# Splitting f32 weights on the engines instead of by summing transfers, in a two-part network kernel

## The chip, the cores and the metric

One core of a Trainium2 chip runs the whole program. Its engines are TensorE (PE, with PEld for weight loads), VectorE (DVE), ScalarE (ACT), GpSimd (POOL) and SyncE (SP), each with an instruction queue that is worked off in order. The metric is the device time of one execution in microseconds, as the median of several runs.

## The reference, cut to what matters

Everything is float32, 256 tokens of width 1024. Two hybrid layers (a gated recurrence beside sparse attention) are followed by one mixer layer (RWKV7 beside a forgetting attention) and a mixture of experts.

```python
def hybrid_layer(x, norm_g, w_in, ..., w_out):          # twice
    h = rms_norm(x, norm_g)
    z = h @ w_in
    ...
    y_a = rg_lru(causal_depthwise_conv(rg_x, conv_w, conv_b), ...)
    y_a = y_a * jax.nn.silu(rg_gate)
    y_b = nsa(q, k_c, v_c, k_s, v_s, k_w, v_w, br_gate, ...)
    y_b = y_b * jax.nn.silu(nsa_gate)
    y = jnp.concatenate([y_a, y_b], axis=-1)
    return x + y @ w_out

def second_block(x, ...):                               # once
    h = rms_norm_2(x, norm_mix_w[l])
    p = h @ w_in[l]
    y_rw = rwkv7_mixer(...); y_fox = fox_mixer(...)
    x = x + jnp.concatenate([y_rw, y_fox], axis=-1) @ w_out[l]
    h = rms_norm_2(x, norm_ffn_w[l])
    return x + hierarchical_moe(h, ...)                 # 16 groups of 4 experts
```

## The kernel before, in words

The dense projections (`h @ w_in`, `y @ w_out`) are computed from split operands: a float32 weight w is turned into hi, which is w rounded to the type that PE reads fast, and lo = w - hi. `mm3_steps` then sums three products, hi by hi, lo by hi and hi by lo (L304). The activations are split by `split` and `split_ps`. What this case is about is where the weights are split.

A weight block is 128 partitions by 2048 columns, 1 MB, half of a chunk of `w_in` or `w_out`. There are 50: blocks 0 to 15 for the first hybrid layer (12 of `w_in`, 4 of `w_out`; the third chunk has only 1120 columns to a half), 16 to 31 for the second, 32 to 49 for the mixer. A split block (hi and lo, 2 MB) lies in one of seven numbered places of SBUF (`block`); `RING` lists the places that blocks go through in turn, and a block's transfer waits until PE has read the block that had its place before. Everything else lies in `arena`, from which `alloc` gives regions out (names in `LONG` from the top).

`weights_steps` is called when a chunk comes up and issues transfers up to a block or two beyond the one it takes:

- Blocks 0 to 3 are loaded as they are by SP into `raw` (L254), ACT writes hi (CAST, L277, in four pieces), and POOL and DVE in turn subtract to make lo (L280).
- From block 4 on, a transfer that POOL issues writes hi and rounds on the way (L256); ACT writes lo = -hi (L286); and two further transfers from POOL read the weights from HBM a second time and add them onto lo (L291, `accum_op=OP.add`).

`hybrid` interleaves the recurrence (`rg_part`) with the attention in small steps on PE (`self.step`). The scan and attention of `mixer` are interleaved in the same manner (the scan's small matmuls are L1057). Softmax work of both attentions is at L801 to L814 on DVE. The mixer's parameters (`par2`, L833) come by SP while the second hybrid layer ends, and DVE scales them at L860 to L863.

The order of instructions on each engine is set by a scheduler from the program, so a step may stand among others' on its queue. `moe` streams the experts' weights, 2 MB at a time, by SP into "slots" (`fill`, L1557 and L1542): the seven places as they come free, and regions of the arena. The first few slots are taken while the mixer still works (`early_slot`), and each waits until what lay there has been read.

Of the kernel before, what the change touches and what calls it, by code (L numbers as in the profile page):

```python
# [35 lines left out]
E_W2, E_G2, E_E8, E_END = 0, 512, 1024, 1536  # L36
ARENA = 24512
BLOCK, NB = 4096, 7
RING = (6, 2, 3, 0, 1)
WS = 2  # L40
# [45 lines left out]
class Net:  # L86
    def __init__(self, ctx, tc, A, norm):
        self.tc, self.nc, self.A = tc, tc.nc, A
        nc = tc.nc
# [6 lines left out]
        self.pool = pool  # L96
        self.blocks, self.loaded, self.nload, self.ntake, self.ndone = [], [], 0, 0, 0
        self.x = self.t([128, 2, 1024], "x")
        for t in range(2):
# [50 lines left out]

    LONG = ("x", "ident", "nh", "cst", "sub", "oneb", "ones", "chunk1", "cmo", "par2", "eh", "small", "fz", "PE",
            "bon", "keyg", "lg", "rss", "gt", "BK", "UV")
# [85 lines left out]
    def plan(self, blocks):  # L238
        self.blocks += blocks
        if self.nload == 0:  # L240
            self.issue(4)

    def issue(self, upto):

        while self.nload < min(upto, len(self.blocks)):
            name, idx, off, n = self.blocks[self.nload][:4]
            b = self.block(RING[self.nload % 5], "w", F32R, 2)[:, :, :n]
            src = self.A[name][idx][:, off:off + n]
            if self.nload < 4:

                if self.nload % 2 == 0:
                    raw = self.block(5 if self.nload else RING[4], "raw", F32, 2)
                src = raw[:, self.nload % 2, :n]
                self.nc.sync.dma_start(src, self.A[name][idx][:, off:off + n])  # L254
            else:
                self.nc.gpsimd.dma_start(b[:, 0], src)  # L256
            self.loaded.append((b, src))
            self.nload += 1

    def weights(self, name, k, pin=False):  # L260
        return run_all(self.weights_steps(name, k, pin))

    def weights_steps(self, name, k, pin=False):


        assert self.blocks[self.ntake][0] == name
        self.issue(self.ntake + 3 - self.ntake % 2)
        i = self.ntake
        b, src = self.loaded[i]
        self.ntake += 1  # L270
        hi, lo = b[:, 0], b[:, 1]
        m = hi.shape[-1]
        r = lambda a: a.rearrange("p (k n) -> p k n", k=k)
        if i < 4:
            for q in range(4):
                sl = slice(q * m // 4, (q + 1) * m // 4)
                a = self.S.copy(hi[:, sl], src[:, sl])  # L277
                if pin:
                    self.tc.keep_in_program_order(a)
                (self.V if q % 2 else self.G).tensor_tensor(lo[:, sl], src[:, sl], hi[:, sl].bitcast(F32), OP.subtract)  # L280
                yield 0
            return r(hi), r(lo)
        n = 4 if m > 1024 else 1
        for i in range(n):
            sl = slice(i * m // n, (i + 1) * m // n)
            a = self.S.activation(lo[:, sl], hi[:, sl].bitcast(F32), AF.Copy, scale=-1.0)  # L286
            if pin:
                self.tc.keep_in_program_order(a)
            if n == 1 or i % 2:
                sl = slice((i - 1) * m // n if i else 0, (i + 1) * m // n)  # L290
                self.G.dma_start(lo[:, sl], src[:, sl], accum_op=OP.add)  # L291
            yield 0
        return r(hi), r(lo)

    def mm3(self, *a):
# [155 lines left out]
    pin = False  # L451
# [270 lines left out]
    def rg_part(self, l, hT, yT, sgn):  # L722
# [27 lines left out]
        self.gated = True  # L750
        tr, ti, a, tq, gt = (self.t([128, 4, 256], n) for n in ("tr", "ti", "a", "tq", "gt"))

# [14 lines left out]
        yield from gates()  # L767
        self.free("xp")

        def out_weights():  # L770
# [71 lines left out]
    def mixer(self, w0, more):  # L842
        nc, T, V, S, G = self.nc, self.T, self.V, self.S, self.G
# [6 lines left out]
        gt = self.t([128, 2, 512], "gt")  # L850
# [22 lines left out]
        lo = self.t([128, 2, 256], "lo", at=12304)  # L873
# [17 lines left out]
        lw, L, ta, k = (self.t(A4, n, at=a) for n, a in (("lw", 4608), ("L", 8192), ("ta", 9216), ("k", 1024)))  # L891
# [327 lines left out]
        for cc in range(4):  # L1219
            i, q = cc // 2, cc % 2  # L1220
# [50 lines left out]
        if more:  # L1271
            self.moe_memory()
            self.moe_params()
            self.route_init()
            self.slots += [self.block(i, "slot", F32) for i in (4, 2, 3)]
            self.fill()
# [400 lines left out]
    def moe(self, out):  # L1677
        ktd = self.t([128, 128], "ktd")
        self.slots += [self.block(i, "slot", F32) for i in ((0, 1, 5) if self.early else range(7))]
        self.fill()  # L1680
# [138 lines left out]
def model(tc, A, out, upto=9, only=None):  # L1819
    with ExitStack() as ctx:  # L1820
# [16 lines left out]
        if only is None:  # L1837
            net.hybrid_params()
            w0 = net.chunk("w_in")
            for l in range(min(2, upto)):  # L1840
                if l == 1:
                    if upto > 2:
                        net.plan_mixer()
                w0 = net.hybrid(l, w0, net.norm_step if l + 1 < upto else None)
            net.free("par", "cl", "ncl", "hb")
        if upto < 3:
# [33 lines left out]
```

## Time and profile before

| what | value |
|---|---|
| median of 3 runs | 1508.16 us (1506.3 to 1509.79) |
| the profiled execution: its own time, its span | 1520.82 us, 1519.1 us |
| PE busy | 1217.5 us, 80% |
| DVE, ACT, POOL busy | 423.2, 316.2, 148.0 us |
| HBM read | 507.83 MB |
| of which through POOL's queue | 90.65 MB |
| mean granted clock of PE | 0.873 of full speed |

Times within the profile belong to the profiled execution, which took 12.66 us longer than the median run. A line L304 is a line of the kernel; an idle time in brackets stands ahead of the instruction that it precedes, with what ended it.

### The profile page before, as it was taken

Reading aid. Unit: us, or ns where it says so; the run is one execution under the profiler, and the core shown is the slowest. Engines: PE = TensorE matmul, PEld = TensorE weight load, DVE = VectorE, ACT = ScalarE, POOL = GpSimd, SP = SyncE. Lnnn points to the kernel's source line nnn. Section 1 sums busy time; section 2 is a strip of 40 time slices with the busy share of each in tenths; the row PEclk is TensorE's granted clock in tenths of the full one; section 3 lists DMA queues with packets and bytes.
Section 4 is the critical chain, followed back from the end, with each engine's and each line's share of the span. In section 5 each row is a group of like instructions: output and inputs, shape, how many; then the busy total and the mean of one; then the engine's idle time right before and its main releaser. Section 6 shows DMA issues by size and latency. Waiting matters only on the chain.

```text
span 1519.1 us, 20669 instructions
## 1 busy us (share of the span) xinstructions
PE 1217.5 (80%) x8695; PEld 678.3 (45%) x8695; DVE 423.2 (28%) x1250; ACT 316.2 (21%) x748; POOL 148.0 (10%) x201
## 2 busy tenths in 40 slices
PE   6799889889778998976876876877868768768774
PEld 5777677676656685431331331322313313313311
DVE  6546346533525465210110101101101101101010
ACT  4448346736223412000000000000000000000000
POOL 5221322122302300000000000000000000000000
PEclk9979989988899898987987888978878979878897
DMA  8976999749746668999999999999999999999996
GB/s 322 229 190 153 254 281 246 196 129 253 177 99 149 158 230 331 428 427 428 428 428 428 428 428 427 427 428 428 427 428 427 427 429 428 427 429 428 423 408 229
DMA packets 62005, 510.27 MB, mean 336 GB/s; under 512 B 5948, under 2 KB 6076, under 8 KB 34388
## 3 DMA queue, kind: packets, MB, share of 16 engines
q1 hardware_dynamic: 42180, 418.26, 65.7%
q0 software_dynamic: 19728, 90.65, 24.7%
q8 instruction: 70, 1.15, 0.3%
q14 instruction: 27, 0.22, 0.0%
HBM read 507.83 MB, written 1.05 MB: 335 GB/s over the span
## 4 chain that ended last, share of the span: by engine, by line
PE 39%; DMA 33%; DVE 3%; issue 3%; POOL 1%; ACT 0%; POOLq 0%; ACTq 0%; DVEq 0%
DMA slot<-in_wu 19%; DMA arena<-in_wu 12%; PE sc L1608 10%; PE ot L1639 8%; PE tp L1579 8%; PE mm L304 5%; DMA arena<-in_wd 1%; PE tp L1630 1%; DVE arena L1626 1%; PE ot L1057 1%; DMA w<-in_w_in 1%; PE mm L1647 0%; POOL w L291 0%; PE sc L1057 0%; PE sc L1374 0%
## 5 line engine op out<-in xcount | busy, mean ns | idle before, releaser
L1608 PE MATMUL sc<-slot,arena 128*32 128x512 f32 x1424 | 326.6, 741 | 132.5 <-DMA slot<-in_wu 81.4
L1608 PE MATMUL sc<-arena 128*32 128x512 f32 x624 | 187.2, 737 | 61.2 <-DMA arena<-in_wu 37.7
L1608 PEld LDWEIGHTS sc<-slot,arena 128*32 128x32 f32 x1424 | 70.0, 131 | 307.6 <-issue 122.5
L304 PE MATMUL mm<-hT,w 128*128 128x256 f32 (+1 forms) x936 | 142.3, 309 | 4.7 <-DMA w<-in_w_in 3.2
L304 PEld LDWEIGHTS mm<-hT,w 128*128 128x128 f32 (+1 forms) x936 | 127.8, 207 | 17.9 <-issue 9.2
L1579 PEld LDWEIGHTS tp<-arena 128*128 128x128 f32 x512 | 124.3, 334 | 17.9 <-issue 17.9
L1579 PE MATMUL tp<-arena 128*128 128x128 f32 x512 | 128.5, 406 | 2.4 <-DVE arena L1577 2.4
L1639 PE MATMUL ot<-slot,arena 128*32 128x512 f32 x704 | 124.4, 596 | 2.8 <-DMA slot<-in_wd 2.0
L286 ACT ACTIVATE w<-w 128x512 fp32r<-128x512 f32 (+1 forms) x181 | 99.0, 603 | 92.5 <-DMA w<-in_w_in 58.1
L1608 PEld LDWEIGHTS sc<-arena 128*32 128x32 f32 x624 | 40.7, 131 | 166.3 <-issue 76.3
L304 PE MATMUL mm<-w,hT 128*128 128x512 f32 (+1 forms) x432 | 105.1, 396 | 10.7 <-DVE arena L502 4.4
L304 PEld LDWEIGHTS mm<-w,hT 128*128 128x128 f32 x432 | 78.5, 200 | 27.8 <-issue 8.8
L1626 DVE SCALAR_TENSOR_TENSOR arena<-arena,sc 128x512 f32<-128x512 f32 x16 | 11.0, 688 | 265.8 <-PE sc L1608 265.8
L1625 DVE SCALAR_TENSOR_TENSOR arena<-arena,sc 128x512 f32<-128x512 f32 x16 | 11.0, 688 | 265.3 <-ACT arena L1624 265.3
L1649 DVE TENSOR_TENSOR arena<-arena,mm 128x512 f32<-128x512 f32 x64 | 44.0, 688 | 118.2 <-PE mm L1647 118.2
L304 PE MATMUL mm<-w,y 128*128 128x512 f32 x288 | 75.5, 408 | 0.9 <-DVE arena L747 0.9
L1639 PE MATMUL ot<-arena 128*32 128x512 f32 x320 | 71.9, 608 | 3.6 <-DMA arena<-in_wd 3.6
L291 POOL DMA_DIRECT2D w<-in_w_in x67 | 59.5, 946 | 136.5 <-ACT w L286 125.5
L1632 ACT COPY arena<-tp 128x512 f32<-128x512 f32 x16 | 9.4, 586 | 302.7 <-PE tp L1630 302.7
L1644 ACT COPY arena<-ot 128x512 f32<-128x512 f32 x32 | 18.8, 586 | 250.3 <-PE ot L1639 250.3
L1647 PE MATMUL mm<-arena 128*128 128x512 f32 x128 | 64.6, 628 | 1.6 <-ACT arena L1644 1.4
L1624 ACT ACTIVATE arena<-sc 128x512 f32<-128x512 f32 x16 | 9.6, 597 | 261.0 <-PE sc L1608 261.0
(386 smaller groups left out, 1246.8 us busy)
## 6 DMA issues: line engine op xcount, KB each, us to landing
slot<-in_wg SPq DMA_DIRECT2D x47, 2048.0 KB, 31.1
slot<-in_wu SPq DMA_DIRECT2D x42, 2048.0 KB, 33.5
slot<-in_wd SPq DMA_DIRECT2D x42, 2048.0 KB, 35.3
arena<-in_wu SPq DMA_DIRECT2D x22, 2048.0 KB, 33.4
arena<-in_wd SPq DMA_DIRECT2D x18, 2048.0 KB, 34.9
arena<-in_wg SPq DMA_DIRECT2D x17, 2048.0 KB, 32.0
w<-in_w_in POOLq DMA_DIRECT2D x29, 1024.0 KB, 8.7
w<-in_w_in POOLq DMA_DIRECT2D x58, 512.0 KB, 8.8
```

What stands on the lines that cost most here:

```text
L286: a = self.S.activation(lo[:, sl], hi[:, sl].bitcast(F32), AF.Copy, scale=-1.0)
L291: self.G.dma_start(lo[:, sl], src[:, sl], accum_op=OP.add)
L304: ins = self.T.matmul(out, lhsT=lhs[k][a], rhs=rhs[k][b], start=(first and i == 0 and k == 0), stop=(last and i == 2 and k == n - 1))
L1057: ins = T.matmul(o[qd(q, d), h * 32:(h + 1) * 32], lhsT=lhs[qd(q, d), h], rhs=rhs[qd(q, d), h], start=True, stop=True)
L1579: ins = T.matmul(self.rows[k // 4][:, k % 4 * 128:(k % 4 + 1) * 128], lhsT=hv[:, tt, k], rhs=D[:, tt], start=(tt == 0 and k % 4 == 0), sto ...
L1608: T.matmul(dst[32 * j:32 * j + 32], lhsT=XT[:, k, 32 * j:32 * j + 32], rhs=w(j), start=(k == 0), stop=(k == 7))
L1626: V.scalar_tensor_tensor(hid, hid, 0.5, pu, OP.mult, OP.mult)
L1630: T.transpose(ps[:, k * 128:(k + 1) * 128], hw[:, k], self.ident)
L1639: T.matmul(py[h][32 * j:32 * j + 32], lhsT=HT[:, k, 32 * j:32 * j + 32], rhs=w(j), start=(k == 0), stop=(k == 3))
L1644: S.copy(Y[:, cs], py[h])
L1647: T.matmul(pc, lhsT=DT[:, tt * 128:(tt + 1) * 128], rhs=Y[:, cs], start=True, stop=True)
L1649: V.tensor_tensor(xs, xs, pc, OP.add)
```

## The change

Every block is now loaded as it is by SP, into one of the two halves of `raw`, which lies in the arena for the two hybrid layers and in place 6 for the mixer. The load of block i+2 is issued only when the instructions that split block i are there (`nload - ndone < 2`), so it waits until block i's half has been read. hi is made by ACT's CAST in four pieces, except in twelve blocks (`by_dma`: 8 to 13 and 24 to 29), where a transfer from POOL writes it. lo is made by subtraction, two quarters on POOL and two on DVE (in the twelve, three on POOL and one on DVE). No transfer adds. The split blocks go through five places in the hybrid layers and four in the mixer. One region (`gt`) is allocated later, the arena grows to hold `raw` (the room comes from a smaller area for POOL's transfer descriptors), and the order in which places become slots for the experts follows the new ring.

```diff
-ARENA = 24512
+ARENA = 26560
-RING = (6, 2, 3, 0, 1)
+RING, RING2, MIXER = (0, 1, 2, 3, 6), (2, 3, 0, 1), 32
...
+        while self.nload < len(self.blocks) and self.nload - self.ndone < 2:
             name, idx, off, n = self.blocks[self.nload][:4]
...
+            if self.nload == MIXER:
+
+                self.raw = self.block(6, "raw", F32, 2)
+            w = self.raw[:, self.nload % 2, :n]
+            self.nc.sync.dma_start(w, self.A[name][idx][:, off:off + n])
...
+    def issue_upper(self, upto):
+
+        while len(self.upper) < min(upto, len(self.blocks)):
...
+            tag = RING[i % 5] if i < MIXER else RING2[(i - MIXER) % 4]
+            b = self.block(tag, "w", F32R, 2)[:, :, :n]
+            if self.by_dma(i):
+                self.nc.gpsimd.dma_start(b[:, 0], self.A[name][idx][:, off:off + n])
...
-            a = self.S.activation(lo[:, sl], hi[:, sl].bitcast(F32), AF.Copy, scale=-1.0)
...
-                self.G.dma_start(lo[:, sl], src[:, sl], accum_op=OP.add)
+            if not self.by_dma(i):
+                a = self.S.copy(hi[:, sl], w[:, sl])
...
+            (self.V if (q == 3 if self.by_dma(i) else q % 2) else self.G).tensor_tensor(lo[:, sl], w[:, sl], hi[:, sl].bitcast(F32), OP.subtract)
             yield 0
+        self.ndone += 1
+        self.issue()
...
+        return i < 32 and 8 <= i % 16 < 14
...
-            self.slots += [self.block(i, "slot", F32) for i in (4, 2, 3)]
+            self.slots += [self.block(i, "slot", F32) for i in (4, 0, 1)]
...
-        self.slots += [self.block(i, "slot", F32) for i in ((0, 1, 5) if self.early else range(7))]
+        self.slots += [self.block(i, "slot", F32) for i in ((2, 3, 5) if self.early else range(7))]
...
+    nc = bacc.Bacc("TRN2", target_bir_lowering=False, num_devices=1, dynamic_dma_scratch_size=8192)
```

Lines after the change stand one or two further on (L304 is L305, L814 is L816); the load is L251, the rounding transfer L263, ACT's CAST L281 and the subtraction L284. Of these the program has 50 loads (one, in the mixer, of only 64 columns), 12 rounding transfers, 152 CASTs, 112 subtractions on POOL and 88 on DVE.

Three places in the queues follow. POOL's queue at the first hybrid layer, before, for blocks 5 to 9 (w_329, w_331, w_373, w_375, w_447):

```order
L256 DMA w_331<-in_w_in 128x2048 [waits PE_49]
L291 DMA w_329<-in_w_in 128x560 [waits Activation_49] x2
L291 DMA w_331<-in_w_in 128x1024 [waits Activation_49]
L291 DMA w_331<-in_w_in 128x1024 [waits DMASW0_49,Activation_49]
L256 DMA w_373<-in_w_in 128x2048 [waits DVE_49,DMASW1_49,PE_49,Pool_49]
L256 DMA w_375<-in_w_in 128x2048 [waits DVE_49,DMASW2_49,PE_49,Pool_49]
L291 DMA w_373<-in_w_in 128x1024 [waits DMASW3_49,Activation_49]
L291 DMA w_373<-in_w_in 128x1024 [waits DMASW4_49,Activation_49]
L256 DMA w_447<-in_w_in 128x2048 [waits DMASW5_49,PE_49]
L256 DMA w_449<-in_w_in 128x2048 [waits DMASW6_49,PE_49]
```

The same stretch of POOL's queue now (block 5 is w_328, 6 is w_329, 7 is w_376, 8 w_377, 9 w_455, 10 w_457, 11 w_743):

```order
L263 DMA w_377<-in_w_in 128x2048 [waits DVE_49,PE_49,Pool_49]
L284 TENSOR_TENSOR w_328<-arena,w_328 128x280 [waits DMAHW4_49,Activation_49]
L284 TENSOR_TENSOR w_328<-arena,w_328 128x280 [waits Activation_49]
L263 DMA w_455<-in_w_in 128x2048 [waits DVE_49,PE_49,Pool_49]
L284 TENSOR_TENSOR w_329<-arena,w_329 128x512 [waits DMAHW5_49,Activation_49]
L284 TENSOR_TENSOR w_329<-arena,w_329 128x512 [waits Activation_49]
L263 DMA w_457<-in_w_in 128x2048 [waits DVE_49,PE_49,Pool_49]
L284 TENSOR_TENSOR w_376<-arena,w_376 128x512 [waits DMAHW6_49,Activation_49]
L284 TENSOR_TENSOR w_376<-arena,w_376 128x512 [waits Activation_49]
L263 DMA w_743<-in_w_in 128x2048 [waits DVE_49,PE_49,Pool_49]
L284 TENSOR_TENSOR w_377<-arena,w_377 128x512 [waits DMAHW7_49,DMASW0_49]
```

The adding transfers are gone; the subtractions of blocks 5, 6 and 7 now each stand behind a rounding transfer that waits for PE to leave a place.

DVE's queue at the end of the second hybrid layer's attention, before (L860 to L862 scale `par2`; L814 divides the last softmax):

```order
L398 TENSOR_TENSOR arena<-arena,mm_2585 128x512 [waits PE_49]
L806 RECIPROCAL arena<-arena 128x4 [waits Activation_49]
L860 TENSOR_SCALAR arena<-arena 128x14 [waits DMAHW1_49]
L809 TENSOR_TENSOR arena<-arena 128x2 [waits DVE_49]
L809 TENSOR_TENSOR arena<-arena 128x2
L861 TENSOR_SCALAR arena<-arena 128x8
L814 TENSOR_SCALAR arena<-arena 128x128 [waits DVE_49]
L814 TENSOR_SCALAR arena<-arena 128x256
L814 TENSOR_SCALAR arena<-arena 128x128 [waits DVE_49]
L814 TENSOR_SCALAR arena<-arena 128x256
L862 TENSOR_SCALAR arena<-arena 128x4
```

The same place of DVE's queue now (w_2717 is block 31, whose split frees the region that `par2` is loaded into):

```order
L284 TENSOR_TENSOR w_2717<-arena,w_2717 128x512 [waits Activation_49]
L399 TENSOR_TENSOR arena<-arena,mm_2600 128x512 [waits PE_49]
L808 RECIPROCAL arena<-arena 128x4 [waits Activation_49]
L811 TENSOR_TENSOR arena<-arena 128x2 [waits DVE_49]
L811 TENSOR_TENSOR arena<-arena 128x2
L816 TENSOR_SCALAR arena<-arena 128x128 [waits DVE_49]
L816 TENSOR_SCALAR arena<-arena 128x256
L816 TENSOR_SCALAR arena<-arena 128x128 [waits DVE_49]
L816 TENSOR_SCALAR arena<-arena 128x256
L399 TENSOR_TENSOR arena<-arena,mm_2649 128x512 [waits PE_49]
L862 TENSOR_SCALAR arena<-arena 128x14 [waits DMAHW4_49]
```

The division has moved ahead of the instruction that waits for `par2`, and a subtraction of the last block of weights stands ahead of both.

SP's queue at the start of the program, before (`raw` is two tiles of two blocks each):

```order
L100 DMA arena<-in_x 128x1024
L254 DMA raw_70<-in_w_in 128x2048 x2
L254 DMA raw_75<-in_w_in 128x2048 x2
L120 DMA arena<-in_cst 128x1218
L125 DMA arena<-in_par 128x968 [waits DMAHW0_49]
L125 DMA arena<-in_par 128x968 [waits DMAHW1_49]
L521 DMA arena<-in_w_cmp 128x4096 [waits DMAHW2_49]
```

And now:

```order
L101 DMA arena<-in_x 128x1024
L251 DMA arena<-in_w_in 128x2048 x2
L121 DMA arena<-in_cst 128x1218
L126 DMA arena<-in_par 128x968 x2
L251 DMA arena<-in_w_in 128x2048 [waits DMAHW0_49,DMAHW3_49,DVE_49,Pool_49]
L251 DMA arena<-in_w_in 128x2048 [waits DMAHW1_49,DMAHW4_49,DVE_49,Pool_49]
L522 DMA arena<-in_w_cmp 128x4096 [waits DMAHW2_49]
L251 DMA arena<-in_w_in 128x1120 [waits DMAHW0_49,DVE_49,Pool_49]
L251 DMA arena<-in_w_in 128x1120 [waits DMAHW1_49,DVE_49,Pool_49]
```

Two loads of blocks go out at once, and from the third on each waits for the subtractions (DVE and POOL) of the block two before it.

## Rows read from the trace of the kernel before

**Rows 1.** Busy time, clock and transfers in two stretches: us, then each engine's.

```profile
0.00:586.00 586.00, 512.03 (x4885) 404.42 (x4886) 297.36 (x961) 271.56 (x663) 147.98 (x201) 0.91 0.78 208
586.00:1519.00 933.00, 705.43 (x3812) 273.84 (x3811) 125.84 (x289) 44.65 (x85) 0.00 (x0) 0.85 0.99 416
```

**Rows 2.** Timeline of SP: the transfer from which slots load without a break.

```profile
557.96 0.37 SPq L1557 DMA_DIRECT2D slot<-in_wu  x1
```

**Rows 3.** Timeline of PE at four gaps: start, us, instruction [idle before <- releaser].

```profile
28.85 12.76 PE L304 MATMUL mm<-w,hT 128*128 128x512 f32 x48 [3.24 <-DVE arena L502]
...
58.20 1.12 PE L540 MATMUL tp<-arena 128*128 128x128 f32 x4 [5.73 <-DVE arena L410]
...
302.90 1.51 PE L822 MATMUL tp<-arena 128*128 128x128 f32 x6 [5.79 <-DVE arena L814]
...
370.02 0.88 PE L981 MATMUL ot<-arena 128*8 128x256 f32 x2 [3.36 <-ACT arena L921]
```

**Rows 4.** Timeline of ACT ahead of the gap at 58.20, and at 367.54.

```profile
53.40 2.19 ACT L286 ACTIVATE w<-w 128x512 fp32r<-128x512 f32 x4 [7.62 <-DMA w<-in_w_in]
...
367.54 0.63 ACT L286 ACTIVATE w<-w 128x512 fp32r<-128x512 f32 x1 [4.74 <-DMA w<-in_w_in]
```

**Rows 5.** Timeline of DVE ahead of the gaps at 58.20 and at 302.90.

```profile
55.97 0.19 DVE L530 TENSOR_SCALAR arena<-arena 128x48 f32<-128x48 f32 x1 [8.23 <-ACT arena L527]
...
302.17 0.17 DVE L860 TENSOR_SCALAR arena<-arena 128x14 f32<-128x14 f32 x1 [6.08 <-DMA arena<-in_par]
```

**Rows 6.** Groups of instructions by line, 186 to 215 us: busy, mean ns | idle before.

```profile
L304 PE MATMUL mm<-w,hT 128*128 128x280 f32 (+1 forms) x91 | 19.3, 372 | 4.4 <-DMA w<-in_w_in 4.4
...
L304 PE MATMUL mm<-hT,w 128*128 128x256 f32 x19 | 3.3, 316 | 2.6 <-DMA w<-in_w_in 2.1 <-ACT arena L527 0.6
```

**Rows 7.** Groups of PE by line, 402 to 466 us, the scan's matmuls.

```profile
L1057 PE MATMUL ot<-arena 32*32 32x32 f32 x896 | 10.6, 195 | 9.7 <-issue 9.7
...
L1057 PE MATMUL sc<-arena 32*32 32x32 f32 x448 | 6.6, 200 | 7.5 <-issue 7.4
```

**Rows 8.** Busy time in one of the scan's gaps, columns as in rows 1.

```profile
460.50:464.00 3.50, 0.00 (x0) 0.00 (x0) 0.74 (x2) 1.15 (x2) 0.00 (x0) 0.77 1.01 215
```

**Rows 9.** Eight stretches behind such gaps: first, last, and the sum of the eight.

```profile
57.00:62.00 5.00, 3.80 (x18) 3.80 (x19) 3.29 (x12) 2.76 (x6) 2.67 (x4) 0.50 1.03 195
...
462.00:469.00 7.00, 5.00 (x63) 3.69 (x67) 0.69 (x1) 2.78 (x5) 3.09 (x6) 0.53 0.78 142
sum 41.00, PE 34.40 PEld 29.13 DVE 10.45 ACT 9.05 POOL 8.17; mean PE 4.30 PEld 3.64 DVE 1.31 ACT 1.13 POOL 1.02
```

**Rows 10.** Instructions on the tile `raw` (blocks 0 to 3): ns min/median/max, and landing in us.

```profile
L277 ACT CAST w<-raw x16: 610/620/625, 10.6 to 22.7; 128x512 fp32r<-128x512 f32 x16
L280 POOL TENSOR_TENSOR w<-raw,w x8: 1274/1304/1835, 11.3 to 25.5; 128x512 fp32r<-128x512 f32 x8
L280 DVE TENSOR_TENSOR w<-raw,w x8: 678/682/5051, 13.1 to 27.4; 128x512 fp32r<-128x512 f32 x8
...
DMA to landing us min/median/max: 8.4/10.4/14.3
```

**Rows 11.** The page's costliest groups over the span: busy, mean ns | idle before.

```profile
L304 PE MATMUL mm<-hT,w 128*128 128x256 f32 (+1 forms) x936 | 142.3, 309 | 4.7 <-DMA w<-in_w_in 3.2
...
L286 ACT ACTIVATE w<-w 128x512 fp32r<-128x512 f32 (+1 forms) x181 | 99.0, 603 | 92.5 <-DMA w<-in_w_in 58.1
...
L291 POOL DMA_DIRECT2D w<-in_w_in x67 | 59.5, 946 | 136.5 <-ACT w L286 125.5
```

**Rows 12.** Timeline of DVE beside POOL's subtractions and products, and alone.

```profile
22.31 5.05 DVE L280 TENSOR_TENSOR w<-raw,w 128x512 fp32r<-128x512 f32 x1 [1.35 <-ACT w L277]
...
511.49 3.47 DVE L814 TENSOR_SCALAR arena<-arena 128x128 f32<-128x128 f32 x4
...
518.76 1.01 DVE L814 TENSOR_SCALAR arena<-arena 128x128 f32<-128x128 f32 x4
```

**Rows 13.** Timeline of POOL beside the first two of rows 12.

```profile
21.19 3.81 POOL L280 TENSOR_TENSOR w<-raw,w 128x512 fp32r<-128x512 f32 x3
...
512.17 1.27 POOL L1143 TENSOR_TENSOR gn<-gn,arena 128x512 f32<-128x512 f32 x1
```

**Rows 14.** The waits up to 620 us: total us, times, longest.

```profile
POOL w L256 <- PE mm L304: 119.8, 23, 18.1
```

More of the change, by code (lines that the diff above doesn't have):

```diff
@@ L97, in __init__ @@
         self.blocks, self.loaded, self.nload, self.ntake, self.ndone = [], [], 0, 0, 0
+        self.raw, self.upper = self.t([128, 2, 2048], "raw"), []
         self.x = self.t([128, 2, 1024], "x")
@@ L148, in block @@
         return t.rearrange(f"p ({' '.join(ax)}) -> p {' '.join(ax)}", **dict(zip(ax, shape)))
-    LONG = ("x", "ident", "nh", "cst", "sub", "oneb", "ones", "chunk1", "cmo", "par2", "eh", "small", "fz", "PE",
+    LONG = ("raw", "x", "ident", "nh", "cst", "sub", "oneb", "ones", "chunk1", "cmo", "par2", "eh", "small", "fz", "PE",
             "bon", "keyg", "lg", "rss", "gt", "BK", "UV")
@@ L239, in plan, with issue @@
         self.blocks += blocks
[L240 to L245, printed above, removed]
+        self.issue()
+    def issue(self):
+        while self.nload < len(self.blocks) and self.nload - self.ndone < 2:
             name, idx, off, n = self.blocks[self.nload][:4]
[L247 to L257, printed above, removed]
-            self.nload += 1
+            if self.nload == MIXER:
+                self.raw = self.block(6, "raw", F32, 2)
+            w = self.raw[:, self.nload % 2, :n]
+            self.nc.sync.dma_start(w, self.A[name][idx][:, off:off + n])
+            self.loaded.append(w)
+            self.nload += 1
+    def issue_upper(self, upto):
+        while len(self.upper) < min(upto, len(self.blocks)):
+            i = len(self.upper)
+            name, idx, off, n = self.blocks[i][:4]
+            tag = RING[i % 5] if i < MIXER else RING2[(i - MIXER) % 4]
+            b = self.block(tag, "w", F32R, 2)[:, :, :n]
+            if self.by_dma(i):
+                self.nc.gpsimd.dma_start(b[:, 0], self.A[name][idx][:, off:off + n])
+            self.upper.append(b)
     def weights(self, name, k, pin=False):
@@ L263, in weights_steps, with by_dma @@
     def weights_steps(self, name, k, pin=False):
-        assert self.blocks[self.ntake][0] == name
-        self.issue(self.ntake + 3 - self.ntake % 2)
         i = self.ntake
-        b, src = self.loaded[i]
+        assert self.blocks[i][0] == name
+        self.issue_upper(min(i - i % 2 + 3, MIXER) if i < MIXER else i - i % 2 + 2)
+        w, b = self.loaded[i], self.upper[i]
         self.ntake += 1
+        m = w.shape[1]
         hi, lo = b[:, 0], b[:, 1]
[L272 to L277, printed above, removed]
+        for q in range(4):
+            sl = slice(q * m // 4, (q + 1) * m // 4)
+            if not self.by_dma(i):
+                a = self.S.copy(hi[:, sl], w[:, sl])
                 if pin:
                     self.tc.keep_in_program_order(a)
[L280 to L285, printed above, removed]
-            a = self.S.activation(lo[:, sl], hi[:, sl].bitcast(F32), AF.Copy, scale=-1.0)
[L287 to L290, printed above, removed]
-                self.G.dma_start(lo[:, sl], src[:, sl], accum_op=OP.add)
+            (self.V if (q == 3 if self.by_dma(i) else q % 2) else self.G).tensor_tensor(lo[:, sl], w[:, sl], hi[:, sl].bitcast(F32), OP.subtract)
             yield 0
+        self.ndone += 1
+        self.issue()
+        r = lambda a: a.rearrange("p (k n) -> p k n", k=k)
         return r(hi), r(lo)
+    @staticmethod
+    def by_dma(i):
+        return i < 32 and 8 <= i % 16 < 14
     def mm3(self, *a):
@@ L750, in rg_part @@
         self.gated = True
-        tr, ti, a, tq, gt = (self.t([128, 4, 256], n) for n in ("tr", "ti", "a", "tq", "gt"))
+        tr, ti, a, tq = (self.t([128, 4, 256], n) for n in ("tr", "ti", "a", "tq"))
         def gates():
@@ L768, in rg_part @@
         self.free("xp")
+        gt = self.t([128, 4, 256], "gt")
         def out_weights():
@@ L1844, in model @@
                 w0 = net.hybrid(l, w0, net.norm_step if l + 1 < upto else None)
-            net.free("par", "cl", "ncl", "hb")
+            net.free("par", "cl", "ncl", "hb", "raw")
         if upto < 3:
@@ L1868 @@
     from concourse.bass_utils import run_bass_kernel_spmd
-    nc = bacc.Bacc("TRN2", target_bir_lowering=False, num_devices=1)
+    nc = bacc.Bacc("TRN2", target_bir_lowering=False, num_devices=1, dynamic_dma_scratch_size=8192)
     arrays, A = {}, {}
```

## The prediction

> **What bounds the kernel now.** I read the busy times by stage first. Up to 586 us PE is busy 512.0 of 586, and transfers take 0.78 of their time; after it transfers take 0.99 at 416 GB/s and PE 705 of 933 [rows 1]. So there are two programs: dense layers near PE's bound with 74 us of idle PE, and an expert stage bound by its stream. SP's timeline shows where the stream becomes continuous, at 557.96 us [rows 2]. Its first slots wait for the places and regions that the mixer reads last, so whatever ends the mixer earlier starts the stream earlier, and the end follows one to one. What DVE, ACT and POOL do matters only where PE waits for them.
>
> Then I looked at PE's gaps before the experts, and behind each at the engine named. The gap of 5.73 us at 58.20 names DVE [rows 3], but DVE had itself waited 8.23 us for ACT's L527 [rows 5], which stood in ACT's queue behind L286, whose four pieces had waited 7.62 us for a weight transfer [rows 4]. The reader should see that a late weight here stops a queue that other work shares. The second hybrid layer starts with 4.4 + 2.6 = 7.0 us of gaps in front of the projections, nearly all put down to weight transfers [rows 6]. The gap of 5.79 us at 302.90 names DVE's L814; DVE stood 6.08 us in L860, waiting for the mixer's parameters [rows 3, 5]. The gap of 3.36 us at 370.02 names ACT's L921, behind an L286 that waited 4.74 us for weights [rows 3, 4]. In the scan, PE's L1057 loses 9.7 + 7.4 = 17.1 us to nothing that the profile names [rows 7]; in the one gap that I show, PE did nothing for 3.5 us while transfers were busy all the time at only 215 GB/s [rows 8]. Behind such gaps PE's clock stands at its lower level, 1.2 GHz of 2.4 (granted 0.50 to 0.58): eight stretches, 41 us together with 34.4 us of PE work [rows 9].
>
> **The change, part by part, against the profiled execution** (1520.82 us, span 1519.1, 1.7 outside; 12.66 above the median, from which I then take the same difference).
>
> *Removed: the second reading and the two chained transfers.* Before, a block needs a landing, ACT, an issue on POOL and a second landing. ACT gives up 181 L286 (99.0 us) for 136 more CASTs of 0.62 us (84 us), POOL gives up its L291 (59.5 us for 67 of them) [rows 10, 11]. Terms, each with both ends:
> - First layer's start: gaps of 3.24 and 5.73, 8.97 together [rows 3]. The first is DVE's L502 behind a subtraction that took 5.05 us [rows 12]; that can recur, as POOL still subtracts there. The second should mostly go, as ACT's queue no longer stops for a landing that was itself queued behind PE. I take 6 (0 to 9).
> - Second layer's start: 7.0, of which I take 6 (0 to 7): raw loads go out as soon as a half of `raw` is read, not when PE leaves a place.
> - `par2`: the order puts the division ahead of the wait, but the load now goes out only after block 31's split, and L862 still holds DVE afterwards. I take 3 of 5.79 (0 to 5.8).
> - L921: 3 of 3.36 (0 to 3.4), for the same reason as the first two.
> - The scan's unnamed gaps: if they are made longer by the slow adding transfers, some of 17.1 goes. Nothing in the trace says how much; I take 4 (0 to 8.5, half).
> - Clock: the 34.4 us of PE work in rows 9 stood at a mean of about 0.53, so at the upper level they would take 18 and save 16. The gaps don't all go, so half: 8 (0 to 16).
>
> Sum of the gains: 6 + 6 + 3 + 3 + 4 + 8 = 30.
>
> *Added: subtractions.* POOL gets 104 more at 1.30 us, 136 us; DVE 80 more at 0.68, 55 us [rows 10]. Up to 586 us that makes DVE 352 and POOL about 220 of 586, ACT 257 [rows 1], so no engine becomes the bound by its sum. What they cost is where they meet. DVE's subtraction beside three of POOL's took 5.05 us and not 0.68, and DVE's L814 took 3.47 us beside POOL's products and 1.01 without them [rows 10, 12, 13]: 2.46 us lost in one meeting. If none lies on the path the price is nothing, since PE has other steps of the interleaved layers to go on with; if one does, it is 2.46. I take three, one for each layer: 7 (0 to 44, the rival below).
>
> The Trainium skill, "SBUF — State Buffer", section "Who interferes with whom", states this as a rule that speaks against the change: a VectorE instruction with two SBUF inputs contends with a GpSimd instruction that reads SBUF, and for VectorE's 2-port modes it says that the other fully blocks for the whole instruction. By that rule every subtraction on one of the two would wait for one on the other, and the two halves of a split would hardly overlap; the two rows above agree, one of 5.05 us with three on POOL of 3.81 us in all beside it.
>
> *Moved: POOL's order.* The subtractions of blocks 5, 6 and 7 stand behind a rounding transfer that waits for PE to leave a place. Such waits took POOL 119.8 us in 23 times before [rows 14], with L291 behind them. The place of block 8 is that of block 3, which PE leaves when it turns to blocks 4 and 5; block 5 then needs an issue of about 0.9 us (as L291) and two subtractions, while PE still has block 4's products. That is close, so 1.5 us a layer, 3 in all (0 to 8). In the attentions the later places come free a block ahead.
>
> *Moved: loads to SP.* SP's queue is in order, and loads stand behind gains, `w_cmp` and `par2`, which wait little: 1 us (0 to 4). Places, slots and `gt` change names, not the time: the last four blocks of the mixer fill four places as before, and six slots follow them. That costs nothing as long as the stream hides it.
>
> Costs: 7 + 3 + 1 = 11. Net: 30 - 11 = 19 us. Of the profiled execution that gives 1502, of the median 1508.16 - 19 = **1489 us**. With the single ends moved by some third, the likeliest case reaches from 1478 to 1501.
>
> **The rivals.**
> - *Slower by meetings on the shared side of DVE and POOL.* The softmax runs on DVE while POOL subtracts 36 quarters in the two attentions. If every second of them meets DVE on the path, that is 18 x 2.46 = 44 us, against 30 - 4 = 26 of net gain: 1508 + 18 = 1526. It decides from 11 meetings on. For it speak rows 12; against it, that DVE is busy only half of the time in these layers [rows 1] and PE is the engine that waits least.
> - *About the same: two halves of `raw` are too few.* A half is taken for a landing, four CASTs (2.5 us) and the last subtraction (1.3). PE's work per block at a layer's start is 48 matmuls at 142.3 / 936 = 0.152, 7.3 us [rows 11]. At the median landing of 10.4 two halves give a block every 7.1 us, just enough; between median and slowest, at 12.4, every 8.1, 0.8 short, and over the eight blocks at each of three starts 19 us: 1508. At the slowest landing, 14.3, it is 1.75 short, 42 us, and slower [rows 10]. Against it: those four loads were in flight at once beside others, and now only two are.
> - *The whole gain.* All terms at their upper ends (9 + 7 + 5.8 + 3.4 + 8.5 + 16 = 50) less the 4 of POOL and SP: 46, 1462 us. For it speaks that most gaps name one cause; against it, that a gap which goes shows the next one.
>
> **How the numbers follow.** The forecast has 0.60, the whole gain 0.13, too few halves 0.13, meetings 0.14. The time is that of the first: 1489. A range that leaves out the outer half of the whole gain and most of the meetings reaches from 1464 to 1512. A difference below 0.2% (3 us) can't be told from none here. The forecast and the whole gain are faster (0.73); the halves' case, from 1489 to 1531 by its landing, gives 0.05 faster, 0.05 same, 0.03 slower; the meetings 0.01 same and 0.13 slower. Together: 0.78 faster, 0.06 same, 0.16 slower.
>
> **What the profile after would show.** Right: no gap of 5 us at 58, no weight transfer among the waits in front of the second layer's projections, landings of raw blocks of 5 to 9 us, a continuous stream from about 539 us. The clock term is right if the granted clock before the experts rises above 0.91. Wrong by meetings: DVE's L816 or the subtractions with means of twice their 0.25 and 0.68 us, and PE waiting for them in the attentions. Wrong by the halves: ACT's CAST waiting for the transfer of `raw`, and PE for CAST. Wrong altogether if the mixer ends earlier but the stream doesn't, because its slots wait for something else.

## The result, and the profile after

The change made the kernel slower: 1548.26 us (median of four runs, 1539.68 to 1554.25) against 1508.97 for the kernel before on the same chip, a ratio of 1.0259 (95% interval 1.0207 to 1.0311). The forecast was 1489, the range 1464 to 1512.

The first view is SP's timeline again, at the transfer from which slots load without a break ([rows 2] of before had it at 557.96).

```profile
586.84 0.37 SPq L1559 DMA_DIRECT2D slot<-in_wu  x1
```

It comes 28.9 us later, and the span is 28.8 us longer (1547.9 against 1519.1). So the expert stage behind it takes what it took, and the whole loss lies ahead of it. The next view cuts that part into the first hybrid layer, the second, and the mixer up to that transfer (columns as in [rows 1]); first the kernel before, then the changed one.

```profile
8.00:168.87 160.87, 145.86 (x869) 116.80 (x867) 91.82 (x312) 89.39 (x227) 47.78 (x59) 0.90 0.81 222
168.87:330.84 161.97, 140.92 (x886) 112.38 (x887) 81.16 (x289) 84.95 (x216) 39.91 (x54) 0.93 0.87 221
330.84:557.96 227.12, 198.86 (x2983) 154.11 (x2984) 102.19 (x279) 85.23 (x188) 56.59 (x72) 0.89 0.68 170
```

```profile
8.00:177.74 169.74, 146.62 (x862) 115.61 (x861) 128.57 (x332) 75.90 (x201) 61.98 (x53) 0.89 0.49 177
177.74:343.37 165.63, 141.81 (x893) 114.18 (x893) 123.50 (x318) 72.43 (x197) 58.78 (x52) 0.94 0.43 153
343.37:586.84 243.47, 211.53 (x2983) 162.53 (x2984) 148.73 (x309) 84.51 (x188) 70.36 (x60) 0.84 0.26 90
```

The layers are 8.9, 3.7 and 16.4 us longer. Transfers are relieved everywhere (0.81 to 0.49, 0.87 to 0.43, 0.68 to 0.26), ACT has less to do, and DVE went from 275 to 401 us of busy time, 126 more, where 80 more subtractions of 0.68 us are 55. The page's groups say where a part of the rest is:

```profile
L284 POOL TENSOR_TENSOR w<-arena,w 128x512 fp32r<-128x512 f32 (+1 forms) x76 | 104.1, 1391 | 116.9 <-ACT w L281 95.2
...
L284 DVE TENSOR_TENSOR w<-arena,w 128x512 fp32r<-128x512 f32 (+1 forms) x52 | 59.9, 1171 | 5.5 <-ACT w L281 4.0
```

On DVE these subtractions took 1171 ns in the mean, 0.68 us where nothing was beside them. The chain of work that ended last runs through DVE for 12% of the span, where it was 3% before (first the kernel before, then the changed one):

```profile
PE 39%; DMA 33%; DVE 3%; issue 3%; POOL 1%; ACT 0%; POOLq 0%; ACTq 0%; DVEq 0%
PE 45%; DMA 35%; DVE 12%; issue 4%; ACT 2%; POOL 1%; SPq 0%; DVEq 0%; ACTq 0%; POOLq 0%
```

The most striking place is in three timelines: DVE, POOL, and PE's largest gap, with three more of its gaps.

```profile
78.08 7.68 DVE L284 TENSOR_TENSOR w<-arena,w 128x512 fp32r<-128x512 f32 x1
85.69 0.27 DVE L619 TENSOR_TENSOR arena<-arena 15x128 f32<-15x128 f32 x1
...
86.60 0.18 DVE L411 TENSOR_TENSOR arena<-arena 15x32 f32<-15x32 f32 x1
```

```profile
77.82 7.40 POOL L284 TENSOR_TENSOR w<-arena,w 128x512 fp32r<-128x512 f32 x6
```

```profile
86.93 0.25 PE L624 MATMUL tp<-arena 15*128 15x15 f32 x1 [7.28 <-DVE arena L411]
...
151.91 1.30 PE L824 MATMUL tp<-arena 128*128 128x128 f32 x5 [4.73 <-DVE arena L816]
...
220.56 1.12 PE L541 MATMUL tp<-arena 128*128 128x128 f32 x4 [4.55 <-DVE arena L411]
...
307.93 1.11 PE L824 MATMUL tp<-arena 128*128 128x128 f32 x5 [3.65 <-DVE arena L816]
```

One subtraction on DVE stood from 78.08 to 85.7 beside a row of six on POOL, from 77.82 to 85.2. Small steps of the attention (L619 to L411) stood behind it, and PE waited 7.28 us for the last of them.

Such a row is rare. The gap of 4.55 us at 220.56 shows what is common (DVE, then POOL):

```profile
214.63 1.77 DVE L284 TENSOR_TENSOR w<-arena,w 128x512 fp32r<-128x512 f32 x1
216.33 1.24 DVE L531 TENSOR_SCALAR arena<-arena 128x48 f32<-128x48 f32 x1
217.49 0.94 DVE L535 TENSOR_TENSOR arena<-arena 128x768 f32<-128x768 f32 x1
218.47 1.30 DVE L408 TENSOR_TENSOR arena<-arena 128x192 f32<-128x192 f32 x1
```

```profile
214.57 4.98 POOL L284 TENSOR_TENSOR w<-arena,w 128x512 fp32r<-128x512 f32 x3 [0.23 <-DMA arena<-in_w_in]
```

L284, L531 and L408 each stood about 1 us longer than alone (0.68, 0.19 and 0.35 us), and POOL's three subtractions took 4.98 us where three alone take 3.9. The two engines took turns, each holding the other for about an instruction. The other two gaps are less clear. Ahead of 151.91 one pair on DVE (L811) took 1.29 us instead of 0.23, and ahead of 307.93 nothing on DVE was held: it worked through steps of the recurrence and the softmax without a break. Whether earlier holds had pushed that work there is not shown.

In the mixer the engines take turns too: of the ten us from 393 to 403, DVE counts as busy for all, with 7 instructions, and POOL for 9.85, with 5, while PE worked 5.18. Only two of POOL's five are subtractions; the other three are products (L1004, L1006) that the kernel before has as well.

```profile
393.00:403.00 10.00, 5.18 (x42) 4.58 (x40) 10.00 (x7) 2.83 (x6) 9.85 (x5) 0.88 0.00 0
```

What the prediction feared of the transfers did not come: blocks land in 4.9 us at the median, 10.0 at most, and ACT waits for them under 9 us in all.

```profile
DMA to landing us min/median/max: 3.6/4.9/10.0
```

### The profile page after: what moved, and what is told of

It is laid out like the page before. It is cut to its first block, busy times and chain, and to the rows that moved or that the text cites. A ratio compares the mean times of both kernels' runs of the same rounds, so it can differ in the third digit from the quotient of the medians.

```text
span 1547.9 us, 20716 instructions
## 1 busy us (share of the span) xinstructions
PE 1228.1 (79%) x8695; PEld 687.9 (44%) x8695; DVE 549.7 (36%) x1330; ACT 289.9 (19%) x703; POOL 194.5 (13%) x180
## 4 chain that ended last, share of the span: by engine, by line
PE 45%; DMA 35%; DVE 12%; issue 4%; ACT 2%; POOL 1%; SPq 0%; DVEq 0%; ACTq 0%; POOLq 0%
DMA slot<-in_wu 18%; DMA arena<-in_wu 12%; PE mm L305 10%; PE sc L1610 9%; PE ot L1641 8%; PE tp L1581 7%; DVE w L284 3%; DMA slot<-in_wg 2%; PE sc L688 1%; PE tp L824 1%; DMA arena<-in_wd 1%; DMA arena<-in_w_in 1%; PE ot L702 1%; PE tp L1632 1%; DMA w<-in_w_out 1%
## 5 line engine op out<-in xcount | busy, mean ns | idle before, releaser
L1610 PE MATMUL sc<-slot,arena 128*32 128x512 f32 x1424 | 321.8, 731 | 135.1 <-DMA slot<-in_wu 82.7
L1610 PE MATMUL sc<-arena 128*32 128x512 f32 x624 | 183.8, 724 | 63.4 <-DMA arena<-in_wu 38.5
L305 PE MATMUL mm<-hT,w 128*128 128x256 f32 (+1 forms) x936 | 143.4, 311 | 2.2 <-DVE arena L873 2.2
L305 PEld LDWEIGHTS mm<-hT,w 128*128 128x128 f32 (+1 forms) x936 | 129.6, 210 | 16.5 <-issue 9.5
L284 POOL TENSOR_TENSOR w<-arena,w 128x512 fp32r<-128x512 f32 (+1 forms) x76 | 104.1, 1391 | 116.9 <-ACT w L281 95.2
L305 PE MATMUL mm<-w,hT 128*128 128x512 f32 (+1 forms) x432 | 103.3, 392 | 7.8 <-DVE w L284 3.0
L305 PEld LDWEIGHTS mm<-w,hT 128*128 128x128 f32 x432 | 78.2, 198 | 24.6 <-DVE w L284 3.9
L305 PE MATMUL mm<-w,y 128*128 128x512 f32 x288 | 76.2, 408 | 0.0
L284 POOL TENSOR_TENSOR w<-raw,w 128x512 fp32r<-128x512 f32 (+1 forms) x36 | 49.8, 1398 | 127.0 <-ACT w L281 118.9
L284 DVE TENSOR_TENSOR w<-arena,w 128x512 fp32r<-128x512 f32 (+1 forms) x52 | 59.9, 1171 | 5.5 <-ACT w L281 4.0
```

The costliest lines, as they stand in the source:

```text
L284: (self.V if (q == 3 if self.by_dma(i) else q % 2) else self.G).tensor_tensor(lo[:, sl], w[:, sl], hi[:, sl].bitcast(F32), OP.subtract)
L305: ins = self.T.matmul(out, lhsT=lhs[k][a], rhs=rhs[k][b], start=(first and i == 0 and k == 0), stop=(last and i == 2 and k == n - 1))
L1610: T.matmul(dst[32 * j:32 * j + 32], lhsT=XT[:, k, 32 * j:32 * j + 32], rhs=w(j), start=(k == 0), stop=(k == 7))
```

## The experiments

The theories, as they went into the expectations: **M**, subtractions on GpSimd and work on VectorE hold each other (the rival "meetings" of the prediction); **L**, VectorE just has too much to do; **R**, the rest of the change (loads, places, order) is slow; later **Q**, GpSimd's time counts because a split ends late, not because VectorE is held. All kernels are edits of the changed one. Ratios are against the kernel before on the same chip.

**No subtraction at all (e1).**

```diff
-            (self.V if (q == 3 if self.by_dma(i) else q % 2) else self.G).tensor_tensor(lo[:, sl], w[:, sl], hi[:, sl].bitcast(F32), OP.subtract)
...
-        return r(hi), r(lo)
+        return r(hi), Mix(r(hi), r(lo), kept)   # reads hi for quarters not in kept
```

> The changed kernel without any subtraction: lo is not made, and PE reads hi in its place, so the loads, the CASTs, the rounding transfers and all matmuls stay and the corrections are left out of the result. Theory M (what the change costs is that subtractions on GpSimd and other work on VectorE hold each other): the gains that the prediction summed become visible, about 1480 us (1470 to 1495). Theory L (VectorE simply has too much to do, meetings or not): the same, 1480, so this run does not tell M from L. Theory R (loads only two ahead, four places in the mixer, the new order of the queues are slow by themselves): 1530 or more.

Measured: 1450.14 us, ratio 0.9603 (0.9544 to 0.9662), below what M and L expected. R falls: without the subtractions the rest of the change saves 4%, some 60 us, twice the 30 that the prediction summed.

**Only VectorE's part (e2) and only GpSimd's (e3).** As e1, with the subtraction kept for the quarters of one engine:

```diff
+            dve = (q == 3 if self.by_dma(i) else q % 2)
+            if dve:                              # e3: if not dve
+                (self.V if dve else self.G).tensor_tensor(lo[:, sl], w[:, sl], hi[:, sl].bitcast(F32), OP.subtract)
+                kept.append(q)
```

> The changed kernel with only VectorE's 88 subtractions; GpSimd's quarters of lo are left out and PE reads hi there. Theory M: VectorE's quarters alone take their 0.68 us each, 60 us in all, most of it beside PE's work: 1485 to 1500. Theory L: the 60 us stand in VectorE's queue ahead of what PE waits for, meetings or not: 1530 to 1545. Theory R: as without subtractions, 1530 or more.

> The changed kernel with only GpSimd's 112 subtractions; VectorE's quarters of lo are left out and PE reads hi there. Theory M: GpSimd's subtractions still meet VectorE's other instructions, so part of the loss stays: 1500 to 1530, with single VectorE instructions held for several us. Theory L: VectorE has nothing added, so about as without any subtraction, 1480 to 1490. Theory R: 1530 or more.

Measured: e2 1474.01, 11 us under M's range, ratio 0.9743 (0.9687 to 0.9798); e3 1512.71, ratio 0.9981 (0.9943 to 1.0019). In per cent of the kernel before, VectorE's 88 cost 1.4 (0.9743 - 0.9603), GpSimd's 112 cost 3.8, and both together 6.6 (1.0259 - 0.9603): 1.4 more than the two apart, which with intervals of about half a per cent on each run is barely clear of the noise. VectorE's part has no subtraction on GpSimd to meet, so its some 24 us (1474 against 1450) are the price of the work in VectorE's queue, with what waits behind it. L falls as the main cause: the larger part comes with GpSimd's part alone, where VectorE has no subtraction to do. In e3's timelines of DVE and POOL, where the program's L740 has become L754 and the subtraction L297:

```profile
58.69 8.33 DVE L754 SCALAR_TENSOR_TENSOR arena<-arena 128x256 f32<-128x256 f32 x2
```

```profile
58.81 7.41 POOL L297 TENSOR_TENSOR w<-arena,w 128x512 fp32r<-128x512 f32 x6
```

Two steps of the convolution that take 0.5 us each stood 8.33 us together beside a row of six. So the subtractions on GpSimd hold other work of VectorE too, not only its subtractions.

**All subtractions on VectorE (e4), all on GpSimd (e5).**

```diff
-            (self.V if (q == 3 if self.by_dma(i) else q % 2) else self.G).tensor_tensor(lo[:, sl], ...)
+            self.V.tensor_tensor(lo[:, sl], ...)        # e5: self.G
```

> The whole computation, with all 200 subtractions on VectorE and none on GpSimd. Theory M: VectorE has 136 us of subtractions before the experts and not 60, but nothing that holds it: faster than the changed kernel, 1500 to 1530. Theory L: VectorE's load more than doubles: slower than the changed kernel, 1570 or more. Theory R: about the changed kernel, 1540 to 1555.

> The whole computation, with all 200 subtractions on GpSimd and none on VectorE. Theory M (GpSimd's subtractions hold VectorE's other instructions; the run with GpSimd's part alone took 1513 where none took 1450): 200 x 1.30 = 260 us of GpSimd against 146, so the loss of 63 grows with it, 1450 + 63 x 200 / 112 = 1562 or more. Rival Q (only the late end of a split counts, since GpSimd takes 1.30 us where VectorE takes 0.68, in a queue of its own): the split of a block takes 5.2 us on one engine, still under PE's 7.3 us a block, so about as with GpSimd's part alone, 1510 to 1530.

Measured: e4 1475.73, ratio 0.9756 (0.9698 to 0.9815), faster than either kernel and than M expected, where L had 1570 or more; e5 1583.39, ratio 1.0497 (1.0449 to 1.0545), above M's bound and far from Q's. On VectorE alone a subtraction takes its own time; in the two groups of e4, min/median/max in ns:

```profile
L284 DVE TENSOR_TENSOR w<-arena,w x128: 437/683/693, 12.8 to 274.3; 128x512 fp32r<-128x512 f32 x112, 128x280 fp32r<-128x280 f32 x16
L284 DVE TENSOR_TENSOR w<-raw,w x72: 166/682/1753, 286.9 to 462.0; 128x512 fp32r<-128x512 f32 x68, 128x16 fp32r<-128x16 f32 x4
```

In the hybrid layers the longest of 128 is 0.69 us; what remains at 1753 is in the mixer, where GpSimd has products of its own.

**The same time on GpSimd, without its reading (e6).** This tells M from Q. As e3, but:

```diff
-                self.G.tensor_tensor(lo[:, sl], w[:, sl], hi[:, sl].bitcast(F32), OP.subtract)
+                s0 = slice(sl.start, sl.start + min(16, m // 4))
+                self.G.tensor_tensor(lo[:, s0], w[:, s0], hi[:, s0].bitcast(F32), OP.subtract)
+                self.G.memset(lo[:, sl].bitcast(F32), 0.0)
+                self.G.memset(lo[:, sl].bitcast(F32), 0.0)
```

> The changed kernel with VectorE's quarters left out as before (PE reads hi there), and on GpSimd in place of each subtraction a subtraction of 16 columns and two writes of a constant over the quarter, which take about as long together (0.24 + 0.52 + 0.52 = 1.28 us) and which PE waits for in the same way, but read SBUF only for the 16 columns; GpSimd's quarters of lo are left out with it. Theory M: VectorE is no longer held, about as without any subtraction, 1450 to 1465. Rival Q: GpSimd's time and its queue are the same, so about as with GpSimd's part alone, 1500 to 1520.

Measured: 1461.28, ratio 0.9674 (0.9632 to 0.9716), where e3 with real subtractions has 0.9981 and e1 with none 0.9603. Most of what GpSimd's part costs goes when it writes for the same time instead of reading, with PE waiting for it in the same manner. Q falls.

**A write behind the subtractions (e9).**

```diff
+            if not (q == 3 if self.by_dma(i) else q % 2):
+                self.G.memset(w[:, sl], 0.0)            # the quarter of raw just read
```

> The changed kernel as it is, and behind each of GpSimd's subtractions (by the order of its queue often behind two of them) one write of a constant over the quarter of raw that it has just read: 0.52 us on GpSimd, which reads no SBUF; the result is the same. Theory row (a held VectorE instruction waits until GpSimd stops reading, so a row of subtractions holds it to the row's end, as one of 7.68 us beside six of 7.40 us in all suggests): the writes let VectorE in, holds stay under some 3 us, and the time falls in spite of 58 us more work on GpSimd: 1515 to 1540. Theory one (a held instruction waits for the one that runs on GpSimd, and the long ones come from something else): the same as the changed kernel or slower, 1545 to 1565.

Measured: 1542.24, between the two ranges, ratio 1.0232 (1.0173 to 1.0291), which can't be told from the changed kernel's 1.0259. The time decides for neither theory, as GpSimd also had 58 us more to do. The timelines of POOL and DVE show what the writes did:

```profile
69.30 2.51 POOL L284 TENSOR_TENSOR w<-arena,w 128x512 fp32r<-128x512 f32 x2
71.76 0.97 POOL L286 MEMSET arena<- 128x512 f32 x2
```

```profile
69.35 3.01 DVE L284 TENSOR_TENSOR w<-arena,w 128x512 fp32r<-128x512 f32 x1
```

With rows of two (2.51 us) and writes behind them, the subtraction that had been held 7.68 us beside six was held 3.01: the two, and its own time. The longest of VectorE's subtractions fell from 7684 ns to 3010, and yet the time stayed; whether a gain is hidden behind GpSimd's added work, this run can't say (e10 below can). Waiting to a row's end is not the rule: in the changed kernel's trace, where one read on GpSimd followed another without a break and a VectorE instruction stood held, it got in between them 41 times and was passed over 8 times; these 8 belong to only three held instructions. What decides between the two is open.

**Without the rounding transfers, all on VectorE (e7) and as changed (e10).**

```diff
-        return i < 32 and 8 <= i % 16 < 14
+        return False
```

> The whole computation with all subtractions on VectorE and hi always by ScalarE: no rounding transfer, GpSimd has no part in the weights. Theory M says nothing of the rounding transfers; if GpSimd's waits for PE ahead of them cost what the prediction gave them (3 us), or if ScalarE's 48 further CASTs of 0.62 us (30 us, amid the attentions) cost nothing, this is 1470 to 1476; if ScalarE's CASTs stand ahead of what the attention waits for, 1480 to 1495.

> The changed kernel without its twelve rounding transfers: ScalarE makes hi of every block, and GpSimd and VectorE each take half of every block's subtractions (100 each, against 112 and 88); the result is the same. If the rounding transfers are slow by themselves, as with all subtractions on VectorE (1476 with them, 1459 without): 1530 to 1536. If what they cost hangs on the subtractions of the same blocks, three of four of them on GpSimd in the changed kernel, more comes back, since 12 of GpSimd's 112 go too: 1515 to 1530. If they matter only where VectorE makes all of lo: 1542 to 1552.

Measured: e7 1459.32, ratio 0.9697 (0.9630 to 0.9764), below both ranges expected; e10 1528.33, ratio 1.0117 (1.0097 to 1.0138), in the second. Without GpSimd's subtractions e7 is 16 us below e4 by the medians, but by the ratios only 0.6% (0.9756 to 0.9697), with intervals that overlap, so that this alone doesn't show that the transfers cost more than the 48 further CASTs. With GpSimd's subtractions the ratio falls by 1.4%, clear of the noise, but e10 has twelve fewer of those, so its 20 us are not the transfers' alone. e7 is the fastest version that computes everything. Its three stretches, cut at the same points:

```profile
8.00:150.98 142.98, 136.62 (x894) 111.28 (x893) 121.73 (x382) 89.69 (x230) 3.35 (x6) 0.99 0.45 166
150.98:282.01 131.03, 125.88 (x861) 101.81 (x861) 109.22 (x348) 82.33 (x215) 3.17 (x6) 1.00 0.41 146
282.01:496.71 214.70, 197.31 (x2983) 152.27 (x2984) 140.01 (x341) 84.66 (x188) 25.88 (x28) 0.91 0.28 102
```

DVE is busy for 371 us here with 200 subtractions, against 401 with 88 in the changed kernel; PE's clock is at its upper level almost throughout both hybrid layers (0.99 and 1.00, before 0.90 and 0.93), and the stretches are 17.9, 30.9 and 12.4 us shorter than before.

**The mixer's products off GpSimd too (e8).** As e7, with L1004, L1006 and L1141 to L1147 on VectorE:

```diff
-        G.tensor_tensor(k, k, kf, OP.mult)
+        V.tensor_tensor(k, k, kf, OP.mult)
```

> The version with all subtractions on VectorE and hi by ScalarE (1459 us), with the mixer's eleven elementwise products on GpSimd (two on 128x1024 in all, the others on 512 columns) moved to VectorE too; the result is the same. Theory M: about 20 us of GpSimd's reading in the mixer become 9 us on VectorE; two places where VectorE stood 1.7 to 1.9 us per instruction of 0.68 lie on the path, so 2 to 6 us faster, 1453 to 1457. Rival: the products stand in VectorE's queue ahead of what PE waits for, and what was parallel becomes serial: 1459 to 1466.

Measured: 1462.01, ratio 0.9728 (0.9663 to 0.9793): no difference from e7's 0.9697 that these runs can tell. VectorE's L997 falls from 3.50 us for two (e7) to 1.30, but L1004 (1.22) and L1006 (0.68 each) now stand in the same queue:

```profile
324.62 1.30 DVE L997 SCALAR_TENSOR_TENSOR arena<-arena 128x512 f32<-128x512 f32 x2
325.84 1.22 DVE L1004 TENSOR_TENSOR arena<-arena 128x1024 f32<-128x1024 f32 x1
326.97 1.22 DVE L998 SCALAR_TENSOR_TENSOR arena<-arena 128x1024 f32<-128x1024 f32 x1
```

A few products in a place where both engines are wanted were worth as much on one as on the other.

**How often VectorE was held.** e10 and e7 differ only in who subtracts (100 and 100, or all 200 on VectorE), and they lie 69 us apart. But e10 has no long row: its longest subtraction on VectorE took 1.78 us, the changed kernel's 7.68. First the changed kernel, then e10:

```profile
L284 DVE TENSOR_TENSOR w<-arena,w x52: 438/694/7684, 12.3 to 312.5; 128x512 fp32r<-128x512 f32 x44, 128x280 fp32r<-128x280 f32 x8
L284 DVE TENSOR_TENSOR w<-arena,w x64: 436/685/1784, 11.9 to 303.6; 128x512 fp32r<-128x512 f32 x56, 128x280 fp32r<-128x280 f32 x8
```

So the holds were counted over each trace up to the continuous stream. Held is a VectorE instruction that took at least 0.3 us longer than the shortest of the same line and shape in any run; every one of them stood beside work on GpSimd.

| kernel | instructions held | longer by, us in all | longest, us | median time, us |
|---|---|---|---|---|
| before | 8 | 13 | 5.05 | 1509 |
| changed | 99 | 101 | 7.68 | 1548 |
| e9, a write behind each | 103 | 98 | 3.01 | 1542 |
| e10, 100 and 100, no rounding transfer | 95 | 91 | 2.90 | 1528 |
| e4, all on VectorE | 7 | 7 | 2.90 | 1476 |
| e7, all on VectorE, no rounding transfer | 8 | 8 | 2.90 | 1459 |

A hold lasted about 1 us in the mean. From the changed kernel to e4, 94 us of holds went and 72 us of time; from e10 to e7, 83 and 69. Some 0.8 of each us held came through to the end, an estimate from these two pairs, in both of which VectorE also took on more work. So the long rows are not what the change mainly costs; the many short holds are.

## Why the prediction was wrong

**The step that failed** is "Added: subtractions". I took "three, one for each layer: 7 (0 to 44, the rival below)" and the runs showed 98 us for all subtractions (1548 against 1450). GpSimd's part alone is 63 (e3 against e1). Some 72 of the 98 are meetings, gone when VectorE does all of it (e4), and some 26 stay there (9 in e7, without the rounding transfers). Three things in it were wrong.

*The count.* This was the main one. I took three meetings; 99 VectorE instructions were held, against 8 before. I thought that PE "has other steps of the interleaved layers to go on with". But its queue is in order too, and the attention's steps alternate between PE and VectorE: 7.28 and 4.55 us in the gaps shown stand behind held instructions, and DVE's part of the chain that ended last went from 3% to 12%. How many of the 99 lie on the path no run says.

*The price.* For one meeting I used 2.46 us from [rows 12]. That was too much, not too little: the row is four instructions of L814, of which three were held, by 0.6 to 1.0 us each, and the mean hold in the changed kernel is 1.0 us. The 5.05 us of the same group were a rare case, and I misread it: beside it stood not three of POOL's instructions but those three, an issue of a transfer (0.58 us) and a fourth subtraction (1.27). Rows of that sort came twice in the changed kernel (7.68 and 4.75 us). And "if none lies on the path the price is nothing" put subtractions that meet nothing at nothing, where e2, with 88 subtractions and no meeting between them and GpSimd's, took 24 us more than none.

*The sum as evidence.* That VectorE would be busy 352 of 586 us counted its own durations only. It was busy 401 in its three stretches, since held time counts as busy.

**The rule of the Trainium skill** that I had set beside the rows ("SBUF — State Buffer", section "Who interferes with whom") is that a VectorE instruction with two SBUF inputs contends with a GpSimd instruction that reads SBUF. The trace agrees: of 67 such instructions that began inside one of GpSimd's in the changed kernel, 65 were held, and e3's L754 and the subtractions are of that kind. e6 agrees as well: reading replaced by writing brought 0.9981 to 0.9674. In the prediction it stood beside the rival "meetings", with 0.14 and 1526 us; the time was 22 us beyond that.

**The rivals.** "Slower by meetings" is what happened, with its place right (the attentions) and the mixer left out, which lost most, 16.4 us. "Two halves are too few" fell: a landing took 4.9 us and not 10.4. "The whole gain" was too small: 46 us, where e1 shows some 60.

**The gains**, step by step. The direction was right and the sum half of what it is. The gap of 5.73 at 58.20 [rows 3] left 0.99 and 2.21 in the changed kernel, and none that the timeline shows at that place in e7. At the second layer's start no wait for weights is left, but the gap of 4.55 us there now names DVE's L411. The wait for `par2` [rows 5] is gone. The scan's 17.1 us [rows 7] fell to 8.4 in the changed kernel, put down to nothing as before, and to 8.1 in e7, so 9 came back where I took 4:

```profile
L1059 PE MATMUL ot<-arena 32*32 32x32 f32 x945 | 11.6, 197 | 7.6 <-issue 7.6
...
L1059 PE MATMUL sc<-arena 32*32 32x32 f32 x512 | 6.7, 199 | 2.7 <-DVE arena L1050 1.8 <-issue 0.8
```

The largest miss among the gains is the clock, of which I took 8 (0 to 16) from eight stretches behind gaps [rows 9]: in e7 PE's busy time in the two hybrid layers is 24 us shorter than before for the same matmuls, at a granted clock of 0.99 and 1.00 instead of 0.90 and 0.93. The changed kernel itself had 0.89 and 0.94 there, so it got little of this. I had counted only stretches behind gaps that I had a cause for.

**POOL's order and the loads.** SP's queue cost nothing that shows. The rounding transfers were put at 3 us (0 to 8); e4 to e7 gives 16 by the medians and 9 by the ratios, not clear of the noise. What they cost, and by which path, is open: GpSimd waits for PE and for VectorE ahead of them, and a block's subtractions wait for them, but no run separates these.

**What would show it** was named rightly in the main: VectorE's subtractions had means of 1.17 and 1.11 us (hybrid layers and mixer), 1.7 times 0.68, and PE waited for VectorE in the attentions. L816 was a poor sign: its mean was 0.38 us, and L814's before had been 0.35, not the 0.25 that it takes alone.

## What to carry to other kernels

Work split between VectorE and GpSimd because both have free time can be slower than all of it on VectorE: 200 subtractions on VectorE gave 1476 us, 88 and 112 gave 1548, 200 on GpSimd 1583. Before dividing, look in the trace of before for VectorE instructions that are longer than others of their kind, and see what GpSimd did beside them. Then price the meetings by their number: count the instructions of these kinds that will stand beside GpSimd's reads, at about the length of one of GpSimd's instructions each (here about 1 us), and don't judge by the one longest hold, which was the easiest to see and counted for little. And an engine's share of busy time says little here, as the time in which it is held is in it.

## What the runs showed of the hardware that was not expected

Which VectorE instructions were held beside GpSimd's subtractions and products is nearly all or none. Of those that began inside one, in the changed kernel, 65 of 67 with two inputs in SBUF were held and 18 of 18 TENSOR_SCALAR, but none of 35 with an input in PSUM.

A hold was mostly over after one of GpSimd's instructions, and then VectorE held GpSimd in turn. But it could last a whole row: 7.68 us beside six of 7.40 us in all, 3.01 beside two of 2.51, and once, before, across an issue of a transfer.

GpSimd's writes held something too. In e6 none of 29 instructions with two inputs in SBUF that began inside a write was held, but 7 of 11 TENSOR_SCALAR were. One of 128x30, 0.17 us elsewhere, took 2.96 us while GpSimd wrote constants six times in a row, from 68.10 to 70.97; e6 is 11 us slower than e1, so all of this counted for little.

```profile
68.05 2.96 DVE L619 TENSOR_SCALAR arena<-arena 128x30 f32<-128x30 f32 x1
```
